# Scan rows by VectorE 32x32 transposes and a round trip through DRAM in a Mamba-2 / short-conv layer on one Trainium2 core

## The chip, the cores and the metric

The kernel runs on one core of one Trainium2 chip. A core has TensorE (PE in the profile, with its weight loads as PEld), VectorE (DVE), ScalarE (ACT), GpSimd (POOL) and SyncE (SP). SyncE issues nearly all DMAs here, in the order in which they stand in its queue: a DMA that waits for data holds up every DMA behind it. The other engines also work through their own queues in order. The metric is device time in microseconds; the kernel before takes 1826.06 us (median of 3 runs, 1825.46 to 1826.92).

## The reference

One layer of a hybrid decoder trunk is applied to 272 prompt positions (16 meta tokens and 256 prompt tokens) and to 8 samples of 8 tokens each, 336 token columns in all. Cut to the part that matters:

```
h = rms_norm(x);  proj = h @ w_in                  # 2048 -> 22592 columns, fp32
z, xbc, dt, sc_b, sc_c, sc_h, sc_z, g_a, g_b = split(proj)
xbc = silu(causal_dwconv4(xbc) + bias)             # xs: 64 heads x 64, B and C: 8 groups x 128
dt = softplus(dt + dt_bias);  log_a = -dt * exp(a_log)
# chunked scan, per group g of 8 heads; chunks of 16, 128, 128 rows and 8 rows for each sample
cb[i,j]  = C[i] . B[j]                             # C.B of a chunk
y_diag   = sum_j cb[i,j] * decay[i,j] * dt[j] * xs[j]
state    = sum_j to_end[j] * dt[j] * xs[j] x B[j]  # carried on from chunk to chunk
y_off[i] = C[i] . h_in * exp(acum[i])              # h_in: the state that enters the chunk
y = y_diag + y_off + d_skip * xs;  y = group_rms_norm(y * silu(z));  y_a = y @ w_ssd_out
y_b = (sc_b * conv3(sc_c * sc_h) * silu(sc_z)) @ w_sconv_out
out = x + (sigmoid(g_a) * y_a + sigmoid(g_b) * y_b) @ w_o
```

A final RMSNorm follows; the conv and scan states are outputs too.

## The kernel before, in words

Activations stand with features on the partitions and the 336 tokens on the free axis, so each weight matrix is split into blocks of 128 output features. Such a **unit** (`unit`, lines 108 to 116) takes two halves of 1024 weight columns (512 KB each). For each half `wblk` (lines 90 to 97) loads `wraw` by SyncE (L92), rounds it to `whi` on ScalarE (L94) and forms the rest `wlo = wraw - whi` on VectorE (L96); `mm` then issues 8 pairs of matmuls with `whi` (L111 for the high part of the activations, L112 for their low part) and 8 with `wlo` (L115). A unit is thus 48 matmuls. `wraw`, `whi` and `wlo` have three buffers each: a load can go out only when VectorE has made `wlo` of the load three before it, and that in turn needs a free `wlo`, so that the loads run up to six halves ahead of TensorE.

The scan runs in eight groups of 8 heads. For each group six units give B, C and four tiles of xs (`x0` to `x3` below); `conv_tile` (L457 to L471) applies the width-4 conv, on ScalarE, GpSimd and VectorE, and writes the tile `BT`, `CT` or `xs[:, t]`, features on the partitions. Four more units give the gate z (`z0` to `z3`), and eight blocks of `w_ssd_out` (L739) project the group before. `ssd(g)` is a generator of 23 steps that `weave` lays between the units of the same stretch: the scan of group g runs while TensorE works on z of group g, on the output projection of group g-1 and on B, C and xs of group g+1. `behind` and the framework's scheduler settle the final order: each engine's queue is written by a scheduler that places an instruction by its own estimate of when it is ready, SyncE's DMAs included.

The scan needs xs and B with rows (tokens) on the partitions too. `rows(c)`, once for each of three row chunks (128, 128 and 80 rows), transposes the four xs tiles on TensorE (L531) and B (L533) into PSUM, and multiplies C.B there (L534). VectorE makes `xdt` (xs times dt, L536) and the masked `cbm` (L548) out of PSUM; ScalarE and VectorE split B into two parts (L543, L544). Later L632 multiplies the eight samples' C (in `CZ`, 32 columns for a pair) with their states `h0`, VectorE scales the result by `eaY` (L635), four TensorE transposes bring it back to features on the partitions (L646), and L652 adds it to `ys`. L642 is the scan's main product, L708 the samples' state update.

Of the kernel before, what the change touches and what calls it, by code (L numbers as in the profile page):

```python
# [38 lines left out]
def fb(ap):  # L39
    return ap.bitcast(F32)  # L40
# [7 lines left out]
def tile_hybrid_step(ctx, tc, xT, w0, w1, w2, wdt, wso, wsc, wo, cmask, vec, hvec, convst, sconvst, xe_, fwe, h0T,  # L48
# [13 lines left out]
    bq_d = [dr.tile([80, 4, P], F32, name=f"bq_d{i}") for i in range(2)]  # L62

# [101 lines left out]
    eaY = keep.tile([P, NH], F32, name="eaY")  # L165
# [4 lines left out]
    with tc.tile_pool(name="pa", bufs=2) as pa:  # L170
# [99 lines left out]
        consts(0, C_SE)  # L270
# [58 lines left out]
        def tables(pt):  # L329
# [94 lines left out]
            nc.tensor.matmul(pc[:, 0:NH], CM[:80, C_SE:C_SE + P], eat[:80, 2, :], start=True, stop=True)  # L424
            nc.vector.tensor_copy(eaY, pc[:, 0:NH])
# [17 lines left out]
    with tc.tile_pool(name="pb", bufs=2) as pb:  # L443
# [4 lines left out]
        CZ = pb.tile([P, 256], F32, name="CZ", bufs=1)  # L448
        nc.gpsimd.memset(CZ, 0.0)
        czs = CZ.rearrange("p (q w) -> p q w", w=64)  # L450

        def conv_tile(src, j, t0, out, cs):
# [12 lines left out]
            for k in range(1, 4):  # L465
# [8 lines left out]
                acc[:, 272:360].rearrange("p (b t) -> p b t", t=11)[:, :, 3:11], add, mult)  # L474

        def conv_units(g, st):
            cs = pb.tile([P, 6, 9, 3], F32, name="cs")
            nc.sync.dma_start(cs, convst[:, g])
            BT = st["BT"] = pb.tile([P, T], F32, name="BT")
            conv_tile(w1[64 + g], 32 + g, 0, BT, cs[:, 4])  # L480
# [4 lines left out]
            xs = st["xs"] = pb.tile([P, 4, T], F32, name="xs", tag=f"xs{g % 2}", bufs=1)  # L485
# [23 lines left out]
        def ssd(g, st):  # L509
            BT, CT, xs = st["BT"], st["CT"], st["xs"]  # L510
            for s_ in range(2):
                nc.gpsimd.tensor_copy(czs[:, :, 40 * s_:40 * s_ + 8],
                                      CT[:, 272:336].rearrange("p (q w) -> p q w", w=16)[:, :, 8 * s_:8 * s_ + 8])
            free = pb.tile([P, 4 * T], F32R, name="xw", tag=f"xs{(g + 1) % 2}", bufs=1)
# [3 lines left out]
            W, xdt, xe, bt, cbm, hst = ([None] * 3 for _ in range(6))  # L518
# [8 lines left out]
            def rows(c):  # L527
                (t0, n), m = CH[c], NT[c]
                pp = ps.tile([P, 512], F32, name="ms")
                for t in range(4):  # L530
                    nc.tensor.transpose(pp[:n, t * P:t * P + P], xs[:, t, t0:t0 + n], ident)  # L531
                pq = ps.tile([P, 512], F32, name="ms")
                nc.tensor.transpose(pq[:n, 0:P], BT[:, t0:t0 + n], ident)  # L533
                nc.tensor.matmul(pq[:n, P:P + m], BT[:, t0:t0 + n], CT[:, TGT[c]:TGT[c] + m], start=True, stop=True)  # L534
                xdt[c] = big("xdt", 3)
                nc.vector.tensor_tensor(split(xdt[c][:n]), split(pp[:n]), bc(hv(dtt[:n, c, :], g), [n, 8, HP]), mult)  # L536
                if c == 2:
                    bt[c] = pb.tile([P, P], F32, name="bt", bufs=1)
                    nc.scalar.activation(bt[c][:n], pq[:n, 0:P], AF.Copy)
                else:  # L540
                    bt[c] = (free[:, 1024:1280].rearrange("p (i n) -> p i n", n=P) if c else
                             pb.tile([P, 2, P], F32R, name="bh0", bufs=1))
                    nc.scalar.activation(bt[c][:, 0, :], pq[:, 0:P], AF.Copy)  # L543
                    nc.vector.tensor_tensor(bt[c][:, 1, :], pq[:, 0:P], fb(bt[c][:, 0, :]), sub)  # L544
                cbm[c] = pb.tile([P, PX], F32, name="cbm")
# [489 lines left out]
```

## Time and profile before

| what | value |
|---|---|
| median of 3 runs | 1826.06 us |
| span of the profiled execution | 1824.0 us (2.06 us under the median) |
| TensorE busy | 1817.0 us, 12640 instructions |
| VectorE, ScalarE, GpSimd busy | 1136.7, 828.8, 374.8 us |
| DMA | 331.35 MB, queue of SyncE 54.6% of 16 engines' span |
| mean granted TensorE clock | 0.999 |

A row of the timeline gives start, duration, engine, line, operation, output<-inputs, shape and count; matmuls overlap, so the distance between starts is what one costs, not its duration. A row of the waits gives who waited, at which line, for whom and where, then the total, the times and the longest. "SPq" is SyncE's queue issuing a DMA, and its duration is the time of the issue alone.

### The profile page before, as it was taken

The page shows a single profiled execution, that of the slowest core. Times are in us where ns is not written, and L with a number is a line of the kernel's source. Part 1 is how long each engine was busy: PE and PEld are TensorE (multiplying, and loading weights), DVE is VectorE, ACT ScalarE, POOL GpSimd, SP SyncE. Part 2 cuts the span into 40 slices and gives each one's busy share as a digit, 9 for nine tenths or more (in the row PEclk, how much of TensorE's full clock was granted, in tenths as well). Part 3 has the DMA queues.
Part 4 walks back from the last instruction along what each step waited for, and adds up shares of the span by engine and source line. Part 5 has one row for each costly group of instructions (what it writes and reads, how often), then busy time and mean ns, then how long its engine had stood idle before and what let it go on. Part 6 is the DMA issues. An engine that isn't in the chain of part 4 may idle for free.

```text
span 1824.0 us, 31666 instructions
## 1 busy us (share of the span) xinstructions
PE 1817.0 (100%) x12640; PEld 1791.5 (98%) x12640; DVE 1136.7 (62%) x1687; ACT 828.8 (45%) x1269; POOL 374.8 (21%) x406
## 2 busy tenths in 40 slices
PE   9999999999999999999999999999999999999998
PEld 9999999999999999999999999999999999999998
DVE  7745544444543335657587787876868778776544
ACT  6433333333333334645656354564536546343543
POOL 0000000000000001143152432424334242400012
PEclk9999999999999999999999999999999999999999
DMA  7444444444444446456566574665746657576553
GB/s 256 143 152 150 151 149 149 144 152 152 156 152 161 162 162 224 151 182 230 168 201 225 174 248 150 205 215 178 244 150 217 201 167 252 159 236 213 183 176 127
DMA packets 117283, 331.35 MB, mean 182 GB/s; under 512 B 20816, under 2 KB 37904, under 8 KB 117136
## 3 DMA queue, kind: packets, MB, share of 16 engines
q1 hardware_dynamic: 116272, 327.96, 54.6%
q8 instruction: 99, 1.62, 0.3%
q10 hardware_dynamic: 864, 1.38, 0.2%
q14 instruction: 48, 0.39, 0.1%
HBM read 296.41 MB, written 32.88 MB: 181 GB/s over the span
## 4 chain that ended last, share of the span: by engine, by line
PE 98%; ACT 1%; DMA 0%; issue 0%; DVE 0%; POOLq 0%; POOL 0%; ACTq 0%; DVEq 0%
PE pj L111 30%; PE pj L112 30%; PE pj L115 30%; PE yb L642 2%; PE pj L219 1%; PE ms L632 1%; PE yb L582 1%; PE pj L857 1%; PE ms L531 1%; DMA wraw<-w 0%; PE ms L219 0%; PE yb L708 0%; PE yb L883 0%; PE ms L646 0%; PE ms L188 0%; ACT W L556 0%
## 5 line engine op out<-in xcount | busy, mean ns | idle before, releaser
L111 PE MATMUL pj<-hx,whi 128*128 128x320 f32 (+3 forms) x2880 | 864.2, 312 | 0.0
L112 PE MATMUL pj<-hx,whi 128*128 128x320 f32 (+3 forms) x2880 | 860.6, 311 | 0.0
L96 DVE TENSOR_TENSOR wlo<-wraw,whi 128x1024 fp32r<-128x1024 f32 x470 | 591.3, 1259 | 417.3 <-PE pj L115 214.8
L94 ACT ACTIVATE whi<-wraw 128x1024 fp32r<-128x1024 f32 x470 | 497.0, 1058 | 773.7 <-PE pj L112 639.6
L111 PEld LDWEIGHTS pj<-hx,whi 128*128 128x128 f32 x2880 | 540.7, 188 | 3.8 <-ACT pad L457 1.7
L112 PEld LDWEIGHTS pj<-hx,whi 128*128 128x128 f32 x2880 | 541.5, 188 | 0.1
L115 PE MATMUL pj<-hx,wlo 128*128 128x320 f32 (+3 forms) x2880 | 485.4, 310 | 0.0
L115 PEld LDWEIGHTS pj<-hx,wlo 128*128 128x128 f32 x2880 | 440.5, 188 | 0.0
L111 PE MATMUL pj<-yh,whi 128*128 128x320 f32 x512 | 153.5, 312 | 0.1
L112 PE MATMUL pj<-yl,whi 128*128 128x320 f32 x512 | 152.2, 308 | 0.0
L593 POOL TENSOR_TENSOR h<-h,decS 128x512 f32<-128x512 f32 x64 | 72.5, 1166 | 152.2 <-PE ms L632 152.2
L111 PEld LDWEIGHTS pj<-yh,whi 128*128 128x128 f32 x512 | 96.6, 189 | 1.4 <-ACT zs L498 0.4
L112 PEld LDWEIGHTS pj<-yl,whi 128*128 128x128 f32 x512 | 95.9, 187 | 0.6
L115 PE MATMUL pj<-yh,wlo 128*128 128x320 f32 x512 | 95.7, 309 | 0.0
L739 DVE TENSOR_TENSOR yan<-yan,pj 128x320 f32<-128x320 f32 x112 | 54.3, 485 | 64.6 <-PE pj L115 63.1
L242 POOL COPY SCS<-up 128x2 f32<-128x2 f32 x16 | 18.2, 1139 | 359.2 <-DVE up L236 329.0
L466 DVE SCALAR_TENSOR_TENSOR cacc<-pad,V,cacc 128x360 f32<-128x360 f32 (+1 forms) x144 | 89.0, 618 | 2.0
L115 PEld LDWEIGHTS pj<-yh,wlo 128*128 128x128 f32 x512 | 80.3, 188 | 0.0
L459 POOL COPY pad<-cs 128x24 f32<-128x24 f32 x48 | 49.5, 1032 | 128.3 <-DVE cacc L466 116.9
L111 PE MATMUL pj<-vhi,whi 128*128 128x320 f32 x256 | 75.5, 308 | 0.0
L112 PE MATMUL pj<-vlo,whi 128*128 128x320 f32 x256 | 75.5, 308 | 0.0
L460 POOL COPY cs<-pad 128x3 f32<-128x3 f32 x48 | 45.3, 944 | 81.5 <-ACT pad L457 81.1
(287 smaller groups left out, 1710.9 us busy)
## 6 DMA issues: line engine op xcount, KB each, us to landing
wraw<-w SPq DMA_DIRECT2D x346, 512.0 KB, 3.8
wraw<-wso SPq DMA_DIRECT2D x64, 512.0 KB, 3.5
wraw<-wsc SPq DMA_DIRECT2D x32, 512.0 KB, 3.7
h<-h0T SPq DMA_DIRECT2D x32, 512.0 KB, 5.5
ssms<-h SPq DMA_DIRECT2D x32, 512.0 KB, 4.3
wraw<-wo SPq DMA_DIRECT2D x32, 512.0 KB, 3.8
xq_d<-xe SPq DMA_DIRECT2D x16, 320.0 KB, 3.4
W<-ac_d SPq DMA_DIRECT2D x8, 576.0 KB, 6.5
```

Source lines behind the costliest of these rows:

```text
L94: latest["act"] = nc.scalar.activation(hi[:, :n], raw[:, :n], AF.Copy).ins
L96: latest["dve"] = nc.vector.tensor_tensor(lo[:, :n], raw[:, :n], fb(hi[:, :n]), sub).ins
L111: nc.tensor.matmul(out, w, xh(k0 + k), start=first and k == 0, stop=False)
L112: nc.tensor.matmul(out, w, xl(k0 + k), start=False, stop=False)
L115: latest["pe"] = nc.tensor.matmul(out, w, xh(k0 + k), start=False, stop=last and k == nk - 1).ins
L219: nc.tensor.matmul(pu[i][:, :T - t0], w[:, o:o + P], x[:, k, t0:], start=k == 0 and j == 0, stop=k == 15 and j == 2)
L459: nc.gpsimd.tensor_copy(smp[:, :, 0:3], cs[:, 1:9, :])
L460: nc.gpsimd.tensor_copy(cs[:, 0, :], pad[:, 272:275])
L466: nc.vector.scalar_tensor_tensor(acc[:, i0:], pad[:, i0 + k:360 + k], col(V_CW, 4 * j + k), acc[:, i0:], mult, add)
L593: nc.gpsimd.tensor_tensor(split(h0[b]), split(h0[b]), bc(hv(decS[:, b, :], g), [P, 8, HP]), mult)
L642: nc.tensor.matmul(yb[q * HP:(q + 1) * HP, t, t0:t0 + n], x[:, h * HP:(h + 1) * HP], w[:, h, :], start=i == 0, stop=i == 3)
L739: nc.vector.tensor_tensor(ya[:, m, :TV], ya[:, m, :TV], pp[:, :TV], add)
```

## The change

Every conv tile of B and xs is transposed by VectorE in blocks of 32x32 (a new L484, in place over the conv's accumulator `cacc`, 128x352 so that 16 leading zeros let the rows start at a block), and four DMAs (L486), one per 32 features, write the blocks as rows of a DRAM tensor `xr_d` (352 rows of 640 columns: 512 of xs, 128 of B), two of which take turns. `ssd` reads the rows back: `xdt` of three chunks (L548) and B (L549). So `rows(c)` loses its 15 TensorE transposes per group; `rows_in(c)` keeps the scaling by dt and the split of B, now from SBUF. `cross()` issues C.B of all three chunks in one step into one PSUM bank (L558) and masks them (L562).

For the samples' outputs the eight products of L632 with 512 columns become 32 with 128 columns (L656), placed so that after the scaling a VectorE 32x32 transpose (of 128x256) gives features on the partitions; the four TensorE transposes of L646 go. `eaY` and `CZ` take the matching layout.

```diff
-        def conv_tile(src, j, t0, out, cs):
...
+        def conv_tile(src, j, t0, out, cs, rows=None):
...
+            if rows:
+                win, to, c = rows
+                nc.vector.transpose(acc[:, :XR], win)
+                for a in range(0, P, 32):
+                    nc.sync.dma_start(to.rearrange("(b q) c -> q b c", q=32)[:, :, c + a:c + a + 32],
+                                      acc[a:a + 32, :XR].rearrange("p (b f) -> p b f", f=32))
...
         def conv_units(g, st):
...
-            conv_tile(w1[64 + g], 32 + g, 0, BT, cs[:, 4])
+            conv_tile(w1[64 + g], 32 + g, 0, BT, cs[:, 4], (BP, to, 512))
...
-                conv_tile(w1[32 + 4 * g + t], 4 * g + t, 0, xs[:, t, :], cs[:, t])
+                conv_tile(w1[32 + 4 * g + t], 4 * g + t, 0, xs[:, t, :], cs[:, t], (xp[:, T * t:T * t + XR], to, P * t))
...
         def ssd(g, st):
...
-            def rows(c):
-                (t0, n), m = CH[c], NT[c]
-                pp = ps.tile([P, 512], F32, name="ms")
-                for t in range(4):
-                    nc.tensor.transpose(pp[:n, t * P:t * P + P], xs[:, t, t0:t0 + n], ident)
-                pq = ps.tile([P, 512], F32, name="ms")
-                nc.tensor.transpose(pq[:n, 0:P], BT[:, t0:t0 + n], ident)
-                nc.tensor.matmul(pq[:n, P:P + m], BT[:, t0:t0 + n], CT[:, TGT[c]:TGT[c] + m], start=True, stop=True)
...
+            rows = xr_d[g % 2][META:]
+            for c, (t0, n) in enumerate(CH):
+                xdt[c] = big("xdt", 3)
+                nc.sync.dma_start(xdt[c][:n], rows[t0:t0 + n, :512])
+                nc.sync.dma_start(bt[c][:n] if c == 2 else fb(bt[c][:, 1, :]), rows[t0:t0 + n, 512:])
+
+            def cross():
                 pq = ps.tile([P, 512], F32, name="ms")
...
+                for c, (t0, n) in enumerate(CH):
+                    m = NT[c]
+                    q = pq[:n, o:o + m]
+                    o += m
+                    nc.tensor.matmul(q, BT[:, t0:t0 + n], CT[:, TGT[c]:TGT[c] + m], start=True, stop=True)
+                    cbm[c] = pb.tile([P, m], F32, name=f"cbm{c}", bufs=1)
...
+                        nc.vector.tensor_tensor(cbm[c][:n, to:to + b - a], q[:, a:b],
+                                                U[:, u0 + a:u0 + b] if c < 2 else UQ[:, a:b], mult)
+
+            def rows_in(c):
+                n = CH[c][1]
+                nc.vector.tensor_tensor(split(xdt[c][:n]), split(xdt[c][:n]), bc(hv(dtt[:n, c, :], g), [n, 8, HP]), mult)
...
-            for s_ in range(2):
-                for q in range(4):
-                    nc.tensor.matmul(po[32 * q:32 * q + 32], CZ[:, 64 * q + 32 * s_:64 * q + 32 * s_ + 32],
-                                     h0[2 * q + s_], start=s_ == 0, stop=s_ == 1)
+            for b in range(NB):
+                z = 160 * (b // 4) + 32 * (b % 4)
+                for a in range(4):
+                    nc.tensor.matmul(po[32 * a:32 * a + 32, P * (b // 4):P * (b // 4) + P], CZ[:, z:z + 32],
+                                     h0[b].rearrange("p (t a f) -> p a t f", a=4, f=32)[:, a],
+                                     start=b % 4 == 0, stop=b % 4 == 3)
...
+            nc.vector.transpose(yo[:, 256:], yo[:, :256])
...
-            for t in range(4):
-                nc.tensor.transpose(pt_[:, t * P:t * P + P], yo[:, t * P:t * P + P], ident)
```

The scheduler writes new queues for all engines. The first place is SyncE's queue where the units x1 to x3 and z0 of a stretch are loaded (`ssmp` and `ssms` are state outputs, `h` the samples' states, `convo` the conv state, `W` the decays of the scan). Number the twenty weight halves of the units B, C, x0 to x3, z0 to z3 from 1 to 20. Before, from halves 9 to 13 on, it reads:

```order
L92 DMA wraw<-w 128x1024 x5
L703 DMA ssmp<-hst 128x512
L714 DMA ssms<-h_8656 128x1024
L714 DMA ssms<-h_8658 128x1024
L604 DMA h_9917<-h0T 128x1024
L604 DMA h_9919<-h0T 128x1024
L92 DMA wraw<-w 128x1024 x4
L524 DMA W<-ac_d_67 128x1152
L489 DMA convo<-cs 128x162
L92 DMA wraw<-w 128x1024
```

and in the changed kernel, from the row writes of tile x1 on:

```order
L486 DMA xr_d_75<-cacc 32x11x32 x4
L739 DMA ssms<-h_8721 128x1024
L94 DMA wraw<-w 128x1024
L486 DMA xr_d_75<-cacc 32x11x32 x4
L739 DMA ssms<-h_8723 128x1024
L739 DMA ssms<-h_8725 128x1024
L507 DMA convo<-cs 128x162
L540 DMA W<-ac_d_67 128x1152
L486 DMA xr_d_75<-cacc 32x11x32 x4
L94 DMA wraw<-w 128x1024 x2
```

Before, halves 14 to 17 stand as one row of four ahead of `convo`, the one DMA here that waits for tile x3 (its cs). In the changed queue half 14 stands behind the row writes of x1, and halves 15 and 16 behind those of x2 and of x3.

The second place is TensorE's queue where unit x3 ends (`pj_9584` before, `pj_9678` in the changed kernel) and z0 goes on (`pj_9669`, `pj_9768`). Before:

```order
L111 MATMUL pj_9584<-hx_80,whi_9617 128x336
L112 MATMUL pj_9584<-hx_80,whi_9617 128x336
L115 MATMUL pj_9584<-hx_80,wlo_9619 128x336 x8
L708 MATMUL yb_9659<-xh_9299,bh_9300 128x512 x4
L111 MATMUL pj_9669<-hx_80,whi_9672 128x320
L112 MATMUL pj_9669<-hx_80,whi_9672 128x320
```

and in the changed kernel:

```order
L113 MATMUL pj_9678<-hx_82,whi_9711 128x336
L114 MATMUL pj_9678<-hx_82,whi_9711 128x336
L117 MATMUL pj_9678<-hx_82,wlo_9713 128x336 x8
L733 MATMUL yb_9758<-xh_9377,bh_9378 128x512 x4
L117 MATMUL pj_9768<-hx_82,wlo_9773 128x320 x8
L113 MATMUL pj_9768<-hx_82,whi_9801 128x320
```

Before, all 48 matmuls of z0 follow x3. Now the 16 with `whi` of z0's first half (half 13) have moved ahead of x3's second half, so 32 of z0 are left behind x3.

The third place is C.B of a group on TensorE, between units z1 and z2. Before, chunk 0 stood there with its transposes (chunks 1 and 2 stood at two later places of the same kind):

```order
L115 MATMUL pj_9746<-hx_80,wlo_9781 128x320 x8
L531 MATMUL ms_9812<-CR_76,xs_9314 128x128 x4
L533 MATMUL ms_9817<-CR_76,BT_9121 128x128
L534 MATMUL ms_9817<-CT_9206,BT_9121 128x112
L111 MATMUL pj_9836<-hx_80,whi_9839 128x320
```

and now all three:

```order
L558 MATMUL ms<-CT,BT 128x112
L113 MATMUL pj<-hx,whi 128x320
L114 MATMUL pj<-hx,whi 128x320
L113 MATMUL pj<-hx,whi 128x320
L114 MATMUL pj<-hx,whi 128x320
L113 MATMUL pj<-hx,whi 128x320
L558 MATMUL ms<-CT,BT 128x144
L114 MATMUL pj<-hx,whi 128x320
L113 MATMUL pj<-hx,whi 128x320
L114 MATMUL pj<-hx,whi 128x320
L113 MATMUL pj<-hx,whi 128x320
L558 MATMUL ms<-CT,BT 80x80
```

The three products stand apart by five and four matmuls of z2; the second and the third wait for VectorE, which reads the product before out of the same PSUM bank.

More of the change, by code (lines that the diff above doesn't have):

```diff
@@ L62, in tile_hybrid_step @@
     bq_d = [dr.tile([80, 4, P], F32, name=f"bq_d{i}") for i in range(2)]
+    xr_d = [dr.tile([XR, 640], F32, name=f"xr_d{i}") for i in range(2)]
     V = keep.tile([P, V_ALL], F32, name="V")
@@ L164, in tile_hybrid_step @@
     eat = keep.tile([P, 3, NH], F32, name="eat")
-    eaY = keep.tile([P, NH], F32, name="eaY")
+    eaY = keep.tile([P, 2, NH // 2], F32, name="eaY")
     cdec = keep.tile([P, 2, NH], F32, name="cdec")
@@ L423, in tables @@
             pc = ps.tile([P, 512], F32, name="ms")
-            nc.tensor.matmul(pc[:, 0:NH], CM[:80, C_SE:C_SE + P], eat[:80, 2, :], start=True, stop=True)
-            nc.vector.tensor_copy(eaY, pc[:, 0:NH])
+            for c in range(2):
+                for a in range(0, P, 32):
+                    nc.tensor.matmul(pc[a:a + 32, NH * c:NH * c + NH], ident[:80, META + 32 * c:META + 32 * c + 32],
+                                     eat[:80, 2, :], start=True, stop=True)
+            for i in range(2):
+                nc.vector.tensor_copy(eaY[64 * i:64 * i + 64], pc[64 * i:64 * i + 64, :2 * NH].rearrange(
+                    "p (c h i) -> p i c h", c=2, i=2)[:, i])
             yield
@@ L474, in conv_tile @@
                 acc[:, 272:360].rearrange("p (b t) -> p b t", t=11)[:, :, 3:11], add, mult)
+            if rows:
+                win, to, c = rows
+                nc.vector.transpose(acc[:, :XR], win)
+                for a in range(0, P, 32):
+                    nc.sync.dma_start(to.rearrange("(b q) c -> q b c", q=32)[:, :, c + a:c + a + 32],
+                                      acc[a:a + 32, :XR].rearrange("p (b f) -> p b f", f=32))
         def conv_units(g, st):
@@ L517, in ssd @@
             ys = pb.tile([P, 4, T], F32, name="ys", bufs=1)
-            W, xdt, xe, bt, cbm, hst = ([None] * 3 for _ in range(6))
+            W, xdt, xe, cbm, hst = ([None] * 3 for _ in range(5))
             W[0], W[1] = (pb.tile([P, 8, PX], F32, name="W")[:, :, :n] for n in (P - META, PX))
@@ L525, in ssd @@
             NT, TGT = (P - META, PX, 80), (META, P, 2 * P)
-            def rows(c):
-                (t0, n), m = CH[c], NT[c]
-                pp = ps.tile([P, 512], F32, name="ms")
-                for t in range(4):
-                    nc.tensor.transpose(pp[:n, t * P:t * P + P], xs[:, t, t0:t0 + n], ident)
-                pq = ps.tile([P, 512], F32, name="ms")
-                nc.tensor.transpose(pq[:n, 0:P], BT[:, t0:t0 + n], ident)
[L534 to L545, printed above, removed]
-                u0 = META if c == 0 else 0
-                for a, b, o in ((0, m, 0),) if c < 2 else ((META, 80, 0), (0, META, 64)):
-                    nc.vector.tensor_tensor(cbm[c][:n, o:o + b - a], pq[:n, P + a:P + b],
-                                            U[:, u0 + a:u0 + b] if c < 2 else UQ[:, a:b], mult)
@@ L595, in ssd @@
             yield
-            rows(0)
+            cross()
             yield
@@ L600, in ssd @@
             nc.scalar.activation(E, W[1], AF.Exp)
-            rows(1)
+            rows_in(0)
             for u in range(4):
@@ L612, in ssd @@
             yield
-            rows(2)
+            rows_in(1)
             yield
```

51 lines of the change are left out of this document (31 added, 20 removed).

## Prediction

> **What bounds the kernel now.** I read the page's sum of engines and the chain that ended last first, then the waits, then the timeline of one group.
>
> ```profile
> span 1824.0 us, 31666 instructions
> PE 1817.0 (100%) x12640; PEld 1791.5 (98%) x12640; DVE 1136.7 (62%) x1687; ACT 828.8 (45%) x1269; POOL 374.8 (21%) x406
> PE 98%; ACT 1%; DMA 0%; issue 0%; DVE 0%; POOLq 0%; POOL 0%; ACTq 0%; DVEq 0%
> ...
> ACT whi L94 <- PE pj L112: 639.6, 315, 4.7
> ACT whi L94 <- DMA wraw<-w: 56.8, 26, 4.9
> SPq L92 <- DVE wlo L96: 1088.3, 412, 9.1
> ```
>
> TensorE never waits: it is busy for the whole span and 98% of the last chain. So time on TensorE counts in full, and so would any new stall of it. The waits show what keeps it fed. ScalarE, which makes `whi`, mostly waits for TensorE to free a buffer (639.6 us), 26 times for a load that is late (at most 4.9 us); SyncE waits for `wlo` before it can load. The feed is ahead, but by a fixed number of buffers.
>
> **What leaves TensorE.** In a timeline of TensorE, the distance between starts is the cost.
>
> ```profile
> 974.29 1.33 PE L115 MATMUL pj<-hx,wlo 128*128 128x320 f32 x8
> 975.46 0.60 PE L531 MATMUL ms<-CR,xs 128*128 128x128 f32 x4
> ...
> 976.00 0.37 PE L534 MATMUL ms<-CT,BT 128*128 128x112 f32 x2
> ...
> 994.57 0.60 PE L531 MATMUL ms<-CR,xs 128*80 128x128 f32 x4
> ...
> 995.12 0.30 PE L534 MATMUL ms<-CT,BT 128*80 128x80 f32 x2
> ...
> 914.94 0.66 PE L646 MATMUL ms<-CR,xe 128*128 128x128 f32 x4
> 915.35 0.40 PE L111 MATMUL pj<-hx,whi 128*128 128x336 f32 x1
> ```
>
> A plain matmul costs (975.46 - 974.29) / 8 = 0.147 us. Four xs transposes and one of B cost 976.00 - 975.46 = 0.54 us in chunk 0 and 0.55 in chunk 2; chunk 1 has the same five. L646 costs 0.41. Per group 0.54 + 0.55 + 0.55 + 0.41 = 2.05 us, for 8 groups **-16.4 us**. C.B stays; its entries too, since the three products stand apart in the new queue.
>
> L656 makes 32 products of 128 columns out of 8 of 512. Both are two records each here:
>
> ```profile
> 909.64 1.92 PE L632 MATMUL ms<-h,CZ 128*32 128x512 f32 x16
> 911.50 0.66 PE L642 MATMUL yb<-W,xdt 128*64 128x112 f32 x8
> ...
> 912.23 0.75 PE L642 MATMUL yb<-W,xdt 80*64 80x80 f32 x12
> 912.81 0.41 PE L642 MATMUL yb<-E,hst 128*64 128x144 f32 x4
> ```
>
> Sixteen records took 1.86 us, 116 ns each; at a quarter of the columns 29 ns, and 64 of them 1.86 us again: no change. From the other side, the shortest records of the trace start 0.58 / 12 = 48 ns apart; 64 x 48 ns = 3.1 us would cost 1.2 us per group, 10 us in all. I take 0, since the column count sets both rows, and keep 0 to +10.
>
> **What is added beside TensorE.** VectorE gets 40 transposes of 128x352 and 8 of 128x256. No row shows one; the cheapest and the dearest VectorE operation of about that width bound it:
>
> ```profile
> L245 DVE TENSOR_SCALAR uc<-up,V 128x336 f32<-128x336 f32 x16 | 6.0, 387 | 0.0
> L354 DVE RECIPROCAL d<-d 64x336 f32<-64x336 f32 x1 | 2.2, 2245 | 0.0
> ```
>
> 0.39 to 2.25 us; I take 0.5, nearer to a plain pass. 48 x 0.5 = 24 us lie on an engine that is busy for 62%: nothing by themselves, under TensorE's cover. SyncE gets 160 row writes and 48 row reads, and these stand ahead of weight loads.
>
> **Where the stall comes from.** The changed queue of SyncE puts the row writes of x1 ahead of half 14, of x2 and x3 ahead of halves 15 and 16. The writes of x3 wait for x3's units on TensorE, its conv on ScalarE and VectorE and the transpose; half 15 waits behind them, though its own buffer has long been free. Before, the same stretch ran so (x3 ends at 960.87 with L708):
>
> ```profile
> 954.85 7.56 SPq L92 DMA_DIRECT2D wraw<-w  x4
> ...
> 960.87 0.50 PE L708 MATMUL yb<-xh,bh 32*128 32x512 f32 x4
> 961.30 0.43 PE L111 MATMUL pj<-hx,whi 128*128 128x320 f32 x1
> ...
> 945.35 0.40 ACT L457 ACTIVATE pad<-pj 128x272 f32<-128x272 f32 x1 [0.23 <-PE pj L115]
> 952.10 0.22 DVE L471 SCALAR_TENSOR_TENSOR xs<-cth,cacc 128x64 f32<-128x64 f32 x1
> 969.21 0.21 DVE L471 SCALAR_TENSOR_TENSOR xs<-cth,cacc 128x64 f32<-128x64 f32 x1
> ...
> wraw<-w SPq DMA_DIRECT2D x346, 512.0 KB, 3.8
> W<-ac_d SPq DMA_DIRECT2D x8, 448.0 KB, 5.8
> L94 ACT ACTIVATE whi<-wraw 128x1024 fp32r<-128x1024 f32 x470 | 497.0, 1058 | 773.7 <-PE pj L112 639.6
> ```
>
> Halves 14 to 17 left SyncE from 954.85 to 962.41, most of them before x3 ended. Now count from the end of x3 on TensorE:
>
> - x3's conv until xs is written: 952.32 - 945.35 = 7.0 us for tile x1, which ScalarE took up at once, and 969.42 - 960.87 = 8.6 for x3, which found ScalarE at other work. I take 7.5.
> - transpose: 0.5, together 8.0.
> - four row writes on SyncE. Their issue has no row; bounds are a plain load and a DMA with a scattered side:
>
> ```profile
> 968.95 0.34 SPq L92 DMA_DIRECT2D wraw<-w  x1
> 908.37 1.90 SPq L665 DMA_DIRECT2D bq_d<-bhh  x2
> ```
>
>   0.34 to 0.95 us each; I take 0.45, as the four follow each other without a wait: 1.8, together 9.8.
> - half 15 lands 3.8 us after its issue (13.6) and ScalarE makes `whi` in 1.06 (14.7).
>
> Meanwhile TensorE has the four L733 (961.30 - 960.87 = 0.43) and the 32 matmuls of z0 behind x3 (32 x 0.147 = 4.7): 5.1 us. It then **stands for 14.7 - 5.1 = 9.6 us**. Conv tiles of a next group are woven into seven of the eight stretches; the first group's run ahead of the loop, where two weight loads stand between the writes of one tile and of the next. So 7 x 9.6 = **+67 us**. Bounds: 7.0 + 0.39 + 1.4 + 3.8 + 1.06 - 5.1 = 8.5, that is +60; and 8.6 + 2.25 + 3.8 + 5.8 + 1.06 - 5.1 = 16.4, that is +115, if all are at their worst at once.
>
> **C.B waits for VectorE.** The second L558 needs the first product read by VectorE. Five matmuls (0.74 us) stand between. In VectorE's new queue that read stands behind two `wlo` and the scaling of the first row chunk:
>
> ```profile
> 971.25 1.22 DVE L96 TENSOR_TENSOR wlo<-wraw,whi 128x1024 fp32r<-128x1024 f32 x1
> ...
> 978.08 0.68 DVE L536 TENSOR_TENSOR xdt<-ms,dtt 128x512 f32<-128x512 f32 x1
> 978.88 0.26 DVE L548 TENSOR_TENSOR cbm<-ms,CR 128x112 f32<-128x112 f32 x1
> ```
>
> If VectorE is free it costs nothing; behind one `wlo`, the scaling and itself, 1.22 + 0.68 + 0.26 - 0.74 = 1.4 us. I take 1.0 for each group, **+8 us** (0 to +11).
>
> **The clock after a stall.** A long stop has a second price:
>
> ```profile
> 1812.00:1818.00 6.00, 5.67 (x51) 5.53 (x49) 3.52 (x7) 0.36 (x2) 3.49 (x3) 1.00 0.51 198
> 1818.00:1824.00 6.00, 0.70 (x4) 0.51 (x4) 1.62 (x3) 0.76 (x2) 1.27 (x1) 0.64 0.64 239
> ...
> 1.24 4.64 PE L188 MATMUL ms<-warm 128*128 128x128 f32 x20 [1.24 <-DVE warm L173]
> 6.36 0.47 PE L219 MATMUL pj<-uhi,whi 128*128 128x322 f32 x1
> 6.63 0.47 PE L219 MATMUL pj<-uhi,wlo 128*128 128x322 f32 x1
> 7.36 0.31 PE L219 MATMUL ms<-uhi,whi 128*128 128x320 f32 x1
> ```
>
> In the last 6 us, with TensorE busy for 0.70, the granted clock is 0.64. At the start matmuls of 322 columns stand 0.27 us apart, where 320 take 0.147 later, and this lasts until about 7.36, 6.1 us after the first. If each stop starts that again, up to 6.1 x (1 - 0.147 / 0.27) = 2.8 us are lost, 20 us in all; if the stop is too short for it, nothing. I take the middle, **+10 us**. The Trainium skill (TensorE: Matmul & The Clock Gate, Part 1: The HAM clock gate) says that the clock halves after an idle window of about 3.4 us and returns after a busy one; by that each stop would lose an estimated 1.7 us, 12 us in all, and the sum would be 2 us higher. The tail row agrees as to the fall, and no row shows the return after a stop of 9.6 us.
>
> **Sum**: -16.4 + 67 + 8 + 10 + 0 = +69 us on the profiled 1824.0, so 1893; the median stands 2.06 us above the span: **1895 us**.
>
> **Rivals.**
>
> *The feed hides it* (faster). If the writes of x3 left SyncE before half 15 is needed, only the -16.4 would stay: 1810 us. For it speaks that the 26 late loads of before, up to 4.9 us, cost TensorE nothing. Against it: z0's 32 matmuls give 5.1 us, and the conv of x3 alone takes 7.0. It would need half 15 loaded ahead of the writes, and the queue does not have it so. From a chain under 5.1 us on, it decides.
>
> *Only the small waits* (no change). Stalls of about 1 us per stretch and the C.B waits give -16.4 + 7 + 8 = -1: 1825 us. It needs the long chain at half its rows.
>
> *The row writes are slow* (slower still). A tile is 4 x 352 packets of 128 bytes. `W<-ac_d` with 1024 packets of 448 bytes lands in 5.8 us against 3.8 for a load of 4 KB packets: 2.0 us for 1024 packets, so 2.8 us for 1408, in front of half 15. With issues at 0.95 each instead of 0.45, 2.0 more: 7 x 4.8 = +34, 1929 us. Against it: both at their bounds. The Trainium skill (DMA: Bandwidth & Descriptors, Specifications) sets 512 bytes as the least transfer for full rate, below which the engine reads, modifies and writes; no run here shows that for writes of 128 bytes. By it this rival is likelier than the rows make it.
>
> *The change does not do what it says* holds in part: C.B is not one visit but three, with two new waits, and this is in the sum.
>
> **Chances.** Forecast 0.76, slow writes 0.15, hidden 0.07, small waits 0.02. The range must leave out no more than 2 in 10: from the lower bounds, -16.4 + 60 + 0 + 0 gives 1870, with 4 us under it for what the walk rounds, and upward past the slow writes to 1938. Within 0.2% (3.7 us) counts as no change: faster 0.07, same 0.02, slower 0.91.
>
> **What would show it.** In the changed profile: TensorE idle at L113, released by ScalarE's `whi`, seven times for 8 to 10 us, and that `whi` waiting for `wraw`; SyncE waiting at L486 for VectorE's transposes; transposes L484 near 0.5 us; L656 at 1.9 us per group; a granted clock below 1 behind each stop. It would be wrong if TensorE stays at 100% of the span, or if the stops hang on another row than x3's.

## The result, and the profile after

The changed kernel takes 1930.86 us (median of 4 runs, 1929.8 to 1933.96) against 1825.76 us of the kernel before on the same chip: ratio 1.0578, 95% interval 1.0563 to 1.0593. It is slower by 105 us. The forecast was 1895 us; the measured time lies 36 us above it and inside the range.

The page of the changed kernel: span, sum of engines, the granted clock in 40 slices, and the DMA packets.

```profile
span 1931.9 us, 32528 instructions
PE 1831.7 (95%) x12886; PEld 1804.6 (93%) x12886; DVE 1186.6 (61%) x1736; ACT 827.6 (43%) x1261; POOL 368.7 (19%) x414
PEclk9999999999999999999989989899899898999999
DMA packets 182312, 345.45 MB, mean 179 GB/s; under 512 B 80592, under 2 KB 100240, under 8 KB 182160
```

TensorE was busy for the whole span before; now it is idle for 100.2 us (1931.9 - 1831.7), 93.2 us more than before. In spite of the transposes that left, it is also busy for 14.7 us more (1831.7 - 1817.0). The two make 107.9 us, the whole difference of the spans. So there are two questions: for what it waits, and why fewer products take longer. The waits answer the first (who waits, for whom; total, times, longest):

```profile
PE pj L113 <- ACT whi L96: 59.5, 7, 9.0
PE ms L558 <- DVE cbm L562: 16.5, 14, 2.5
PE pj L117 <- DVE wlo L98: 14.0, 14, 1.9
PE pj L113 <- DVE yan L764: 3.3, 6, 1.5
ACT whi L96 <- DMA wraw<-w: 121.5, 39, 6.9
SPq L486 <- DVE cacc L484: 94.8, 40, 4.6
```

The first four rows are all of the new idle time. Seven stops of up to 9.0 us hang on `whi`; `whi` waits for the load `wraw`; and SyncE stands 40 times at L486 for VectorE's transpose. One such stop, from the end of x3 on, in the timelines of TensorE, VectorE, SyncE and ScalarE:

```profile
979.17 0.51 PE L733 MATMUL yb<-xh,bh 32*128 32x512 f32 x4
984.28 1.44 PE L117 MATMUL pj<-hx,wlo 128*128 128x320 f32 x8 [0.91 <-DVE wlo L98]
994.28 0.64 PE L113 MATMUL pj<-hx,whi 128*128 128x320 f32 x1 [8.56 <-ACT whi L96]
994.71 0.47 PE L114 MATMUL pj<-hx,whi 128*128 128x320 f32 x1
994.98 0.47 PE L113 MATMUL pj<-hx,whi 128*128 128x320 f32 x1
...
985.66 0.22 DVE L478 SCALAR_TENSOR_TENSOR xs<-cth,cacc 128x64 f32<-128x64 f32 x1
985.92 0.55 DVE L484 STREAM_TRANSPOSE cacc<-xs 128x352 f32<-128x352 f32 x1
...
986.49 1.86 SPq L486 DMA_DIRECT2D xr_d<-cacc  x4
988.45 0.88 SPq L94 DMA_DIRECT2D wraw<-w  x2
...
993.17 1.06 ACT L96 ACTIVATE whi<-wraw 128x1024 fp32r<-128x1024 f32 x1 [6.41 <-DMA wraw<-w]
```

Read it down: x3 leaves TensorE at 979.17; its conv ends at 985.88, the transpose at 986.47; four row writes are issued until 988.35; only then half 15 leaves, ScalarE can take it up 4.7 us later, and TensorE goes on at 994.28. That is the chain of the prediction, on the predicted row.

The second question is answered by windows of the granted clock, the share of its full speed at which TensorE was let run (TensorE's busy time stands first behind the width, the clock is the third number from the end):

```profile
994.00:996.00 2.00, 1.72 (x6) 1.72 (x7) 1.69 (x2) 1.29 (x2) 0.00 (x0) 0.50 1.11 332
996.00:998.00 2.00, 2.00 (x11) 2.00 (x11) 2.00 (x9) 0.00 (x0) 0.00 (x0) 0.68 0.98 306
998.00:1000.00 2.00, 2.00 (x16) 2.00 (x15) 0.27 (x2) 1.70 (x2) 0.00 (x0) 1.00 0.98 373
...
1006.00:1008.00 2.00, 1.09 (x6) 0.83 (x6) 1.97 (x5) 0.38 (x1) 1.04 (x1) 0.88 1.03 418
1008.00:1010.00 2.00, 1.97 (x8) 1.97 (x9) 1.38 (x3) 0.68 (x1) 0.12 (x1) 0.50 0.24 87
1010.00:1012.00 2.00, 2.00 (x12) 2.00 (x12) 0.06 (x1) 1.06 (x1) 0.00 (x0) 0.76 0.29 63
```

Behind the stop the clock is 0.50, and products start 994.98 - 994.71 = 0.27 us apart where 0.147 is usual. It falls a second time from about 1007, behind the two waits for C.B (2.47 us ahead of 1006.32, 0.61 ahead of 1008.03). Busy time times the missing share of the clock is 1.72 x 0.50 + 2.00 x 0.32 = 1.5 us for the first fall and 1.09 x 0.12 + 1.97 x 0.50 + 2.00 x 0.24 = 1.6 us for the second. The same sum over all windows of 1 us from 20 to 1720 is 21.6 us; before it is 0. Of the 21.6, seven falls around the stops cost 15.2 us (1.5 to 3.1 each), and falls behind C.B, in four of the seven groups, 6.4 us (1.4 to 1.7 each).

The added and changed operations themselves, by groups (busy, mean ns of one):

```profile
L484 DVE STREAM_TRANSPOSE cacc<-xs 128x352 f32<-128x352 f32 x32 | 17.2, 537 | 0.3
L656 PE MATMUL ms<-h,CZ 128*32 128x128 f32 x512 | 15.6, 274 | 0.0
xr_d<-cacc SPq DMA_DIRECT2D x160, 44.0 KB, 2.0
```

A VectorE transpose takes 0.54 us. L656 is busy for 15.6 us, as L632 was (15.4). A row write of 44 KB lands 2.0 us after its issue.

### The profile page after: what moved, and what is told of

Read it like the earlier page. It is cut to its first block, busy times and chain, and to the rows that moved or that the text cites. A ratio compares the mean times of both kernels' runs of the same rounds, so it can differ in the third digit from the quotient of the medians.

```text
span 1931.9 us, 32528 instructions
## 1 busy us (share of the span) xinstructions
PE 1831.7 (95%) x12886; PEld 1804.6 (93%) x12886; DVE 1186.6 (61%) x1736; ACT 827.6 (43%) x1261; POOL 368.7 (19%) x414
## 2 busy tenths in 40 slices
DMA packets 182312, 345.45 MB, mean 179 GB/s; under 512 B 80592, under 2 KB 100240, under 8 KB 182160
## 5 line engine op out<-in xcount | busy, mean ns | idle before, releaser
L113 PE MATMUL pj<-hx,whi 128*128 128x320 f32 (+3 forms) x2880 | 874.8, 315 | 59.5 <-ACT whi L96 59.5
L114 PE MATMUL pj<-hx,whi 128*128 128x320 f32 (+3 forms) x2880 | 872.3, 315 | 0.0
L113 PEld LDWEIGHTS pj<-hx,whi 128*128 128x128 f32 x2880 | 549.3, 191 | 64.3 <-ACT whi L96 61.4
L114 PEld LDWEIGHTS pj<-hx,whi 128*128 128x128 f32 x2880 | 550.6, 191 | 0.1
L117 PE MATMUL pj<-hx,wlo 128*128 128x320 f32 (+3 forms) x2880 | 491.9, 313 | 14.0 <-DVE wlo L98 14.0
L615 POOL TENSOR_TENSOR h<-h,decS 128x512 f32<-128x512 f32 x64 | 76.5, 1227 | 86.9 <-PE ms L656 86.9
L466 POOL COPY pad<-cs 128x24 f32<-128x24 f32 x48 | 63.9, 1334 | 139.7 <-DVE cacc L473 133.8
L476 ACT ACTIVATE cth<-cacc 128x360 f32<-128x360 f32 (+1 forms) x48 | 24.1, 501 | 66.6 <-DVE cacc L473 66.6
```

What stands on the lines that cost most here:

```text
L113: nc.tensor.matmul(out, w, xh(k0 + k), start=first and k == 0, stop=False)
L114: nc.tensor.matmul(out, w, xl(k0 + k), start=False, stop=False)
L117: latest["pe"] = nc.tensor.matmul(out, w, xh(k0 + k), start=False, stop=last and k == nk - 1).ins
L466: nc.gpsimd.tensor_copy(smp[:, :, 0:3], cs[:, 1:9, :])
L476: nc.scalar.activation(th[:, i0:], acc[:, i0:], AF.Tanh)
L615: nc.gpsimd.tensor_tensor(split(h0[b]), split(h0[b]), bc(hv(decS[:, b, :], g), [P, 8, HP]), mult)
```

## The experiments

The theory is the prediction's: the stops come from the place of x3's row writes ahead of half 15 in one queue that waits in order. The main rival is that the row writes themselves, 1408 packets of 128 bytes per tile, slow the loads. In kernels with a longer `cross()` the lines behind it stand 5 further down.

### The place in the queue

**The writes on another queue.**

```diff
-                    nc.sync.dma_start(to.rearrange(...)[:, :, c + a:c + a + 32], ...)
+                    nc.gpsimd.dma_start(to.rearrange(...)[:, :, c + a:c + a + 32], ...)
```

> Only the engine that issues the row writes L486 is changed, from SyncE to GpSimd; packets, bytes and the wait for VectorE's transpose stay. Queue theory (half 15 is late because the row writes stand ahead of it in SyncE's queue): the stops at L113 behind whi (59.5 us, seven of 7.6 to 9.0) go, and with them most of the clock loss of some 31 us, say 20; 1930.9 - 59.5 - 20 = 1851 us, within 1840 to 1870, as small waits for wlo may stay. Packet theory (the 1408 packets of 128 bytes of a tile slow the weight loads, whoever issues them): the packets are the same, so the stops at L113 keep more than half of their length, and the time stays above 1895 us.

Measured: 1864.61 us, ratio 1.0213 (1.0199 to 1.0227). TensorE's waits in this run, and its row of packets:

```profile
PE ms L558 <- DVE cbm L562: 33.9, 9, 5.0
PE pj L113 <- ACT whi L96: 0.4, 1, 0.4
...
DMA packets 128553, 345.45 MB, mean 186 GB/s; under 512 B 24272, under 2 KB 43920, under 8 KB 128400
```

The 59.5 us at `whi` are gone, and so are the 14.0 us at `wlo`, with the same bytes. But the packets are not the same, though the expectation took them to be: 56320 of those under 512 B are gone (80592 - 24272), 352 for each of the 160 writes, and a write from GpSimd's queue is recorded as 32 larger packets (5120 in all). So this run fits the queue theory, but it does not rule out the packet rival. The timeline of the changed kernel bounds the rival: half 15 leaves SyncE 9.3 us after the end of x3 (988.45 - 979.17), and of what follows only the landing could be longer by the packets, 4.7 us against 3.8. The next run keeps the packets. The wait for C.B has doubled; that is taken up below.

**The writes later in the same queue.**

```diff
-                for a in range(0, P, 32):
-                    nc.sync.dma_start(to..., acc...)
+                held.append([LATE, write])      # LATE = 4; wblk issues it behind the fourth load from here
```

Two more things differ from the changed kernel: the row reads are issued in step with C.B, and C.B's three products stand ahead of their maskings (as in the next section).

> All row writes stay on SyncE, but each tile's four are held back until four weight loads later, so that two halves more (15 and 16) stand ahead of x3's writes; row reads in step with C.B; C.B's three products ahead of their maskings. Theory (the stop is the place of x3's writes ahead of half 15 in one queue, not what SyncE or the packets cost): the stops of 7.5 to 9 us at L113 go, as they went with GpSimd's queue; the time comes near the 1858 us of that run with the same C.B, 1850 to 1880 us. Rival (SyncE has no time for 160 issues of 0.46 us, 74 us in all, or the packets slow its loads): the loads are late in any order, above 1890 us.

Measured: 1881.65 us, ratio 1.031 (1.029 to 1.033), 2 us outside the range of the theory and 8 below that of the rival. `whi` still holds TensorE up:

```profile
PE pj L121 <- ACT whi L104: 40.1, 15, 4.5
```

No wait is longer than 4.5 us now, where they were 7.5 to 9.0, but there are 15. The packets are those of the changed kernel (182313, 80592 of them under 512 B), and the time is 28 us below the 1909.64 us of the run with C.B in this order and the writes at their old place: the place of the writes and reads in the queue counts, with the packets unchanged. The queue that also feeds the weights stays the worse place: with C.B in this order, the writes on GpSimd's queue leave 16.7 us in 16 waits there, of at most 2.4 us (below).

**Twice as many writes.**

```diff
+                for a in range(0, P, 32):
+                    nc.sync.dma_start(xs_d[npad[0] % 2]..., acc...)      # a second set, read by nobody
```

> Each tile's four row writes are issued twice on SyncE, the second set to DRAM that nothing reads. Theory (a stop is as long as the walk from x3's end, in which an issue on SyncE costs 0.46 us): the stop at L113 grows by 4 x 0.46 = 1.85 us a group, 13 us over seven, and half 15 lands as before, some 4.7 us after its issue: 1940 to 1960 us. Packet theory (1408 more packets of 128 bytes stand in front of half 15 in the DMA engines, 2.0 us for 1024 by the row of W's loads): half 15 lands 2.8 us later besides, + 33 us in all: 1964 us or more.

Measured: 2005.78 us, ratio 1.0984 (1.0969 to 1.0999): more than either expectation. A stop is now 19.1 us. In the timelines of TensorE, SyncE and ScalarE:

```profile
1004.66 0.51 PE L737 MATMUL yb<-xh,bh 32*128 32x512 f32 x4
1024.27 0.63 PE L114 MATMUL pj<-hx,whi 128*128 128x320 f32 x1 [19.10 <-ACT whi L97]
...
1013.14 1.99 SPq L490 DMA_DIRECT2D xs_d<-cacc  x4
1017.03 1.64 SPq L95 DMA_DIRECT2D wraw<-w  x2
...
1023.16 1.06 ACT L97 ACTIVATE whi<-wraw 128x1024 fp32r<-128x1024 f32 x1 [13.29 <-DMA wraw<-w]
```

TensorE stands right behind L733's counterpart: the products of z0 (4.7 us for the 32 of the changed kernel) no longer cover anything, because the scheduler moved the loads of z0 behind the writes too, and TensorE waits for half 13 here. The rest of the growth is the second set of issues (2.2 us), the DMAs (state outputs) that now stand between the writes and this load (1017.03 - 1013.14 - 1.99 = 1.9 us), and a landing of 6.1 us (1023.16 - 1017.03) instead of 4.7. So the run says little of the 1.85 us it was made for. What it does say of the packets: with twice as many, the load lands 1.4 us later than in the changed kernel, and there it landed 0.9 us later than the 3.8 of before. Other transfers were under way as well, so these are bounds: a set of packets costs at most 0.9 to 1.4 us per stop, not 2.8.

### C.B, and VectorE beside GpSimd

**The three products ahead of the maskings.**

```diff
                     nc.tensor.matmul(q, BT[:, t0:t0 + n], CT[:, TGT[c]:TGT[c] + m], start=True, stop=True)
+                o = 0
+                for c, (t0, n) in enumerate(CH):
+                    ...
                     cbm[c] = pb.tile([P, m], F32, name=f"cbm{c}", bufs=1)
```

> In cross() the three C.B products are issued first and the four maskings after them; nothing else, and SyncE's queue keeps its order. Theory (VectorE's masking L562 between two products makes TensorE wait, and the clock falls a second time in each group behind these waits): the 16.5 us of idle time at L558 go and some 1.2 us of half clock in each of seven groups with them: 1930.9 - 16.5 - 8 = 1906 us, within 1900 to 1914; the seven stops at L113 stay at 7.5 to 9 us. Rival (VectorE is late at that place in any case, and TensorE meets the same lateness one step on, at wlo or at the next use of the buffer): the idle time moves to another row, 1922 to 1931 us.

Measured: 1909.64 us, ratio 1.0459 (1.0445 to 1.0473). The row of L558 is gone from the waits, the others stay (`wlo` has 14.3 us in 14 times):

```profile
PE pj L113 <- ACT whi L96: 60.4, 7, 9.0
```

The spans differ by 25.1 us: 16.5 of the wait, and 9.9 less busy time of TensorE (1821.8 instead of 1831.7), less 1.2 that the other waits gained. The theory holds: this wait cost 16.5 us and some 10 us of busy time, 6.3 of it by the clock (21.6 us lost before, 15.3 in this run).

**Why VectorE is late there.** In the changed kernel, VectorE, GpSimd and TensorE around the first of the two waits:

```profile
1002.95 3.14 DVE L567 TENSOR_TENSOR xdt<-xdt,dtt 128x512 f32<-128x512 f32 x1
1006.00 0.26 DVE L562 TENSOR_TENSOR cbm<-ms,CR 128x112 f32<-128x112 f32 x1
...
1002.90 2.63 POOL L589 TENSOR_TENSOR E<-E,CT 128x1152 f32<-128x1152 f32 x1 [17.83 <-ACT E L622]
...
1006.32 0.51 PE L558 MATMUL ms<-CT,BT 128*128 128x144 f32 x2 [2.47 <-DVE cbm L562]
```

The scaling L567 takes 3.14 us where the one before, out of PSUM, took 0.68. It begins when GpSimd's L589 is at work and ends 0.56 us after it. To tell it from a slowdown by transfers, L589 was moved off GpSimd:

```diff
-                    nc.gpsimd.tensor_tensor(E, E, bc(CT[:, P:P + PX].unsqueeze(1), [P, 8, PX]), mult)
+                    nc.vector.tensor_tensor(E, E, bc(CT[:, P:P + PX].unsqueeze(1), [P, 8, PX]), mult)
```

> The changed kernel with one operation moved: E's product L589 on VectorE instead of GpSimd. Theory (VectorE's L567 and L571 read two operands from SBUF since the rows come through DRAM, and such an operation stands while GpSimd works on SBUF: 3.14 us beside L589's 2.63 where it takes 0.68 alone): L567 ahead of the first masking takes 0.68 us, the first wait at L558 (2.5 us a group) goes, the idle time at L558 falls from 16.5 to under 5 us, and the clock falls once a group less: 1905 to 1920 us. Rival (L567 is slow because transfers write to SBUF at the time): L567 stays at some 3 us and L558 keeps its 16.5 us: 1928 us or more, with VectorE some 10 us busier.

Measured: 1916.05 us, ratio 1.0494 (1.048 to 1.0508). The wait at L558 and the group of L567 (24 operations: the mean was 1400 ns):

```profile
PE ms L558 <- DVE cbm L562: 1.0, 2, 0.5
L567 DVE TENSOR_TENSOR xdt<-xdt,dtt 128x512 f32<-128x512 f32 (+1 forms) x24 | 17.2, 717 | 0.0
```

The wait falls from 16.5 to 1.0 us, L567 is as fast as alone. The theory holds. The run with the writes on GpSimd's queue shows the same with another operation, and explains its 33.9 us:

```profile
982.55 2.61 DVE L571 TENSOR_TENSOR bh<-bh 128x128 fp32r<-128x128 f32 x1
...
982.40 2.62 POOL L589 TENSOR_TENSOR E<-E,CT 128x1152 f32<-128x1152 f32 x1 [3.95 <-ACT E L622]
```

A subtraction of 128x128, 0.28 us alone, ends 0.14 us after GpSimd's product, and the first masking stands behind it. The Trainium skill (SBUF — State Buffer, SBUF: two separate sides) says that a VectorE operation with two SBUF inputs and a GpSimd operation that reads SBUF lock each other out for a whole instruction. The trace agrees, with 2.61 us beside 2.62.

### The clock behind a stop

```diff
                 pz = proj(w1[4 * g + t], META)
+                if t == 0:
+                    for _ in range(90):      # into columns of pz's buffer that nothing reads
+                        nc.tensor.matmul(pt[:, 336:], onesR, hhi[:, 0, :176], start=True, stop=True)
```

> The changed kernel with 90 more products of 176 columns behind each z0, in columns of the buffer that nothing reads: some 90 x 0.147 x 176 / 320 = 7.3 us of work, less than the stop of 8.5 us that follows there. Theory (the stop has a second price, since the clock is granted at half after it): behind the filled stop the clock stays at 1, the first products of z1 start 0.147 us apart instead of 0.27, and 7 x 1.35 = 9.5 us go: 1921 us, the end of the stops where it was. Rival (the slow products are the pipeline filling again, or the clock falls by the hour of the stage and not by idleness): 0.27 us apart as before, 1928 us or more. If the added products run at half clock themselves, they take 14.6 us and make the stop longer: above 1960 us.

Measured: 1964.48 us, ratio 1.0758 (1.0744 to 1.0772). The added products, the first products behind them, and the window in which these lie:

```profile
999.50 10.18 PE L512 MATMUL pj<-hx,CR 128*128 128x176 f32 x90
1009.52 0.34 PE L113 MATMUL pj<-hx,whi 128*128 128x320 f32 x1
1009.70 0.31 PE L114 MATMUL pj<-hx,whi 128*128 128x320 f32 x1
1009.85 0.30 PE L113 MATMUL pj<-hx,whi 128*128 128x320 f32 x1
...
1010.00:1012.00 2.00, 2.00 (x16) 2.00 (x15) 2.00 (x9) 0.00 (x0) 0.00 (x0) 1.00 0.87 303
```

Where the stop was filled, the clock stays at 1.00, during the added products too, and the products of z1 start 0.15 us apart from the second on. The slow products are the price of idleness, not of the place in the program: the clock now falls behind the longer waits for C.B (seven times, 16.6 us by the same sum). The time itself lies where the expectation put added products at half clock, but for other reasons: they took 111 ns each and not 81, so 10.0 us instead of 7.3 and more than the stop; the eighth group has them without a stop to fill; and the scheduler laid C.B so that its waits grew to 42.9 us in 8 times.

### The samples alone

The kernel before with L656, `eaY`, `CZ` and the transpose of `yo` as in the changed kernel, and nothing else:

```diff
-            pt_ = ps.tile([P, 512], F32, name="ms")
-            for t in range(4):
-                nc.tensor.transpose(pt_[:, t * P:t * P + P], yo[:, t * P:t * P + P], ident)
+            nc.vector.transpose(yo[:, 256:], yo[:, :256])
```

> The kernel before with the samples' part of the change alone: 32 products of 128 columns for 8 of 512, one VectorE transpose for four TensorE transposes per group; rows of x and B stay on TensorE, no new transfer. Theory: the products cost the same (1.9 us per group) and four transposes leave, 0.41 x 8 = 3.3 us: 1822.5 us, ratio 0.9982. Rival (short products cost at least 48 ns each, the upper bound of the prediction): + 1.2 x 8 = 10 us and - 3.3: 1832 us. The VectorE transpose of 128x256 takes about 0.4 us by the 0.53 us of the 128x352 one, and nothing waits for it.

Measured: 1823.94 us, ratio 0.9991 (0.9982 to 1.0), which can hardly be told from no change; TensorE's row of the sum of engines:

```profile
PE 1814.7 (100%) x13006; PEld 1797.8 (99%) x13006; DVE 1147.7 (63%) x1696; ACT 828.8 (45%) x1269; POOL 388.8 (21%) x398
```

TensorE is busy for 2.3 us less (1817.0 - 1814.7), not 3.3. The rival of 48 ns a product falls.

### Is there a faster version?

**Both remedies**, the writes on GpSimd's queue and the three products first:

> Row writes on GpSimd's queue and C.B's three products ahead of their maskings, together; all else as in the changed kernel. In the run with GpSimd's queue alone the span was 1860.8 us with 33.9 us of idle time at L558 and 1817.2 us of busy TensorE, where 1817.0 - 16.4 = 1800.6 is what the change should leave. Theory (both places are told apart, and the second falls of the clock hang on the waits at L558): the 33.9 us go and most of the 16.6 us of slow matmuls: 1864.6 - 33.9 - 14 = 1817 us, within 1809 to 1826. Rival (VectorE, held up by GpSimd, is late for wlo as well, so the wait moves): 1835 to 1855 us.

Measured: 1858.1 us, ratio 1.018 (1.0166 to 1.0194), 32 us above the theory's range and 3 above the rival's; and the wait did not move to `wlo`, as the rival had it. The 33.9 us at L558 are gone, and in their place stand:

```profile
PE pj L113 <- ACT whi L96: 16.7, 16, 2.4
PE pj L113 <- ACT zs L516: 12.6, 7, 1.9
```

For `zs` TensorE waits until ScalarE comes to it: one was written at 999.42, after 1.93 us of waiting, and ScalarE had worked without a gap from 994.33 on. The weight loads leave SyncE behind the row reads, and SyncE stands there 27 times (59.8 us in all) until the row writes have landed. With **the row reads on GpSimd's queue too** (`nc.gpsimd.dma_start` at L548 and L549):

> The same, and the row reads L548 and L549 leave on GpSimd's queue too. Theory (what is left of the loss is weight loads behind reads that wait on SyncE for the writes of x3 to land): by what it still costs in the run without this, 0 to 8 us faster than it. Rival (GpSimd then stands at the reads for some 2 us, and its products for E, xe and the states come later): 0 to 10 us slower than it.

Measured: 1855.67 us, ratio 1.0165 (1.0152 to 1.0179), 2.4 us faster than without, which the scatter of the two (1853 to 1859 and 1856 to 1862 us) hardly tells from none. The waits at `whi` fall to 2.2 us, so that most of them hung on the reads; those for ScalarE's `zs` grow to 24.2.

**Only the early tiles through DRAM.** First B, x0 and x1, still on SyncE, with C.B's products first and the rows of x2 and x3 by TensorE as before:

```diff
-                conv_tile(..., (xp[:, T * t:T * t + XR], to, P * t))
+                conv_tile(..., (xp[:, T * t:T * t + XR], to, P * t) if t < 2 else None)
```

> Rows of B, x0 and x1 by VectorE transposes and DRAM as in the changed kernel, rows of x2 and x3 by TensorE transposes as before; C.B's three products ahead of its maskings; samples as in the changed kernel. Theory (the row writes of the last two tiles hold halves 15 and 16, those of the first tiles hold nothing that is needed soon): no stop of 7 to 9 us at L113; three fifths of 1.64 us of transposes leave in 8 groups (7.9 us), and 3.3 of the samples: 1825.8 - 11 = 1815 us, up to 1835 if reads that wait for x1's writes hold one load a little. Packet theory: three fifths of the packets are still there, and so three fifths of the loss: about 1880 us.

Measured: 1865.66 us, ratio 1.0212 (1.0197 to 1.0228): between the two expectations. The long stops are gone, but eight shorter ones stay at `whi`:

```profile
PE pj L113 <- ACT whi L96: 24.3, 8, 3.6
...
974.25 2.80 SPq L94 DMA_DIRECT2D wraw<-w  x3
...
981.15 1.06 ACT L96 ACTIVATE whi<-wraw 128x1024 fp32r<-128x1024 f32 x1 [3.24 <-DMA wraw<-w]
```

The half that TensorE needs left SyncE at 974.25 and was there 6.9 us later instead of 3.8, in a stretch where the DMA engines are nearly always busy (0.62 to 1.06 of each 2 us from 972 to 984; state reads, state outputs and loads leave together behind the row reads). Which of these transfers is to blame was not tried alone. Then B and x0 only, with writes on GpSimd's queue and C.B's products first, and the same with L589's product on VectorE:

> Only rows of B and x0, the first tiles of a group, by VectorE transposes and DRAM, their writes on GpSimd's queue; rows of x1 to x3 by TensorE as before; C.B's three products ahead of their maskings; samples as in the changed kernel. Theory (what a tile's writes cost is their place ahead of a half that is needed soon; these tiles are written 20 us and more before their rows are read): no long stop at L113; two of five transposes a chunk leave, 0.4 x 1.64 x 8 = 5.2 us, and the samples' 1.8 as measured: 1825.6 - 7 = 1819 us, up to 1826 with small waits. Rival (any row through SBUF and any work more on GpSimd's queue makes VectorE and the conv late): 1830 to 1850 us.

> The same, with E's product on VectorE, so that no product of two SBUF operands on VectorE stands behind it. If that stand (2.6 us a group) still reaches TensorE in the run without this, it is 3 to 15 us faster than that run; if VectorE had time to spare there, it is within 3 us of it.

Measured: 1833.08 us, ratio 1.0043 (1.0031 to 1.0055), and 1845.39 us, ratio 1.0106 (1.0093 to 1.0119). The first is 7 us above the theory's range and inside the rival's. In it the clock never falls and TensorE is busy for 4.9 us less than before (1812.1 against 1817.0), but it waits:

```profile
PE pj L113 <- ACT zs L517: 7.1, 7, 1.4
PE pj L113 <- DVE yan L775: 3.6, 5, 0.7
```

The second was expected to be no slower and is 12 us slower: with one product of some 1.4 us more per group on VectorE, the wait for its sum `yan` grows from 3.6 to 9.9 us, and the clock falls four times (6.7 us by the same sum). VectorE is busy for 63% of the span, and yet has nothing to spare in these stretches. No version with rows through DRAM came out faster than the kernel before, and the samples' part alone is even with it.

## Why the prediction was right, and where its terms were off

The direction, the mechanism, the row and the number of the stops came out as forecast. Its terms, against the traces:

- **What bounds the kernel**: a stall of TensorE counts in full. Idle and busy time of TensorE account for all of the 107.9 us.
- **The stop, +67**: the walk gave 14.7 us from x3's end to the next product, and 15.1 were measured (994.28 - 979.17). Its parts: conv 6.7 (taken 7.5), transpose 0.6 (0.5), issues 1.9 (1.8), landing 4.7 (3.8), `whi` 1.1. TensorE then stood for 8.56 us and, inside the cover, for 0.91 at `wlo`: together 9.5, against 9.6. That it came out so near is in part luck: the conv was 0.8 us shorter than taken and the landing 0.9 longer. Over the run `whi` and `wlo` make 73.5 us (59.5 + 14.0). Seven of the 14 waits at `wlo` lie inside the stop like the 0.91 (8.1 us). The seven others, 0.84 us each ahead of it, are 5.9 of the 6.5 us that the term lacked, and no step of the walk has them. No load is late there: for the one that ends at 974.02, `whi` had been ready since 960.03, and VectorE worked through other operations without a gap until it began this `wlo` at 972.76. It is the order of VectorE's new queue; the run with the writes on GpSimd's queue has another order there and none of these waits, and the run with only B, x0 and x1 through DRAM keeps seven of at most 0.84 us.
- **C.B, +8**: mis-sized. It measured 16.5 us: 12.2 in the first waits of the seven groups and 4.2 in the second ones (0.6 each), for which the sum had no term. The prediction priced the row scaling in front of the masking with the 0.68 us that it took out of PSUM. The change gives it two operands in SBUF, and beside GpSimd's product it took 3.14. The diff showed the new operand; the step that failed is to take the 0.68 us of the old row for an operation whose operands had moved.
- **The clock, +10**: mis-sized. 21.6 us were lost. Behind the stops it was 15.2 us, 2.2 each where 1.43 were taken, within the bound of 2.8 on average and in five of the seven groups (3.0 and 3.1 in the others); and 6.4 us fell behind the waits for C.B, which the prediction had not counted as stops at all. With C.B's products first, 15.3 us are left, so that the two parts are told apart by a run. The Trainium skill (TensorE: Matmul & The Clock Gate, Part 1: The HAM clock gate) was drawn on for 1.7 us per stop, 12 us in all. The trace agrees as to half the rate; the return came after 3.0 us of work here (994.3 to 997.3), and in another group only after some 6 (1376.9 to 1383). Its idle window of 3.4 us would have had me expect no fall behind C.B: TensorE was idle there for 2.47 us and a little later for 0.61, and the clock fell all the same.
- **Transposes, -16.4**: too much. The samples alone gave 2.3 us of busy time where 3.3 were counted. B's and x0's transposes with the samples' gave 4.9 where 5.2 + 3.3 were counted. The distance between starts of neighbours says what an instruction takes in its place, and some of it stays when it leaves. For the full change the traces leave 14.7 - 21.6 = -6.9 us for the transposes and whatever else the busy time holds. How much of the missing 9.5 us are transposes worth less, and how much the products that fill the pipeline again behind some 40 waits, was not told apart.
- **L656, 0** and **VectorE's transposes under cover**: 15.6 against 15.4 us; 0.54 us against the 0.5 taken. The added 0.54 us do not show on TensorE by themselves.
- **A wait for `yan`, 3.3 us**, was not foreseen.

The sum of the traces: 73.5 + 16.5 + 3.2 (the other waits) + 21.6 - 6.9 = 107.9 us. The forecast's +69 lacked 8.5 at C.B, 11.6 of clock, 6.5 of the stops, 3.2 of other waits and 9.5 of busy time. All of these missed on the slow side. That the range holds the measured time is luck too: its upper end was drawn past the slow writes, and it was not slow writes that brought the time there.

**The rivals.** "The feed hides it" and "only the small waits" fell with the seven stops. "The row writes are slow" named 1929 us and so came nearer to the time than the forecast, for a wrong reason: its 2.8 us of packets per stop measured at most 0.9, its issues at 0.95 us each measured 0.46. The run with the writes held back on SyncE has the same packets and is 28 us faster than the one with the writes at their old place and C.B in the same order. The Trainium skill (DMA: Bandwidth & Descriptors, Specifications) made this rival likelier, with its rule on transfers under 512 bytes. No run here refutes the rule, but its price for the load that follows is at most 0.9 us in the changed kernel. "The change does not do what it says" holds: C.B is three visits, and that was worth 25 us.

## What to carry to other kernels

A DMA that waits for computed data belongs in no queue that also feeds the bounding engine: count from the end of the work that it waits for to the use of the load behind it, and compare with what the engine still has to do. When a change moves an operand from PSUM to SBUF, price the operation anew, and look at what GpSimd does at that time. When a run is to keep the packets and move only the queue, look at its row of packets first. An engine that is busy for 63% of the span may have no slack in the stage where work is added, so look at windows of that stage before anything is called covered.

## What the runs showed of the hardware that was not expected

- VectorE with two SBUF operands stands while GpSimd works on SBUF: 2.61 us for an operation of 0.28, 3.14 for one of 0.68, beside GpSimd's 2.62 and 2.63.
- The clock fell behind 2.47 us and 0.61 us of idleness within 4.2 us. It fell so in the four groups of seven in which the first of these waits was 1.72 to 2.52 us long, and not in the three in which it was 0.66 to 1.48. Behind a single wait of 1.86 us (for `wlo`, ahead of 1112.99) it fell as well, while one of 0.84 us (ahead of 974.02) left it at 1.00. The same stop cost 1.5 us of clock in one group and 3.1 in another.
- A product of 176 columns with the same weights each time starts 111 ns after the one before, not 81: fewer columns do not shorten it in proportion.
- A row write issued on GpSimd's queue holds that engine's queue for 0.63 us (160 of them 99.9 us in all) and lands 4.9 us after its issue, against 0.46 and 2.0 on SyncE's. The same 44 KB are 32 packets on GpSimd's queue (5120 for 160 writes), while from SyncE's they hold 352 packets of under 512 B.
